# Attention's probabilities times values in plain float32, two key blocks in the two column halves of the array

## The chip, the core and the metric

One core of a Trainium2 chip runs the whole layer as one program. The metric is the device time of one execution in microseconds. The kernel before took 1462.4 us in the median of three runs (1460.74 to 1462.71). Engines are named as in the profile: PE is TensorE (PEld its weight loads), DVE is VectorE, ACT is ScalarE, POOL is GpSimd, SP is SyncE, which issues most DMAs.

## The reference, cut to what matters

The layer normalises its input, projects it once, and feeds two groups of heads: a gated delta rule (8 heads, chunks of 64 tokens) and multi-head latent attention (8 heads). Their outputs go through one output projection; a squared-ReLU MLP, a gated per-layer embedding and a final norm follow. There are 1024 tokens and 1024 channels, all float32. The change lies in the attention group:

```python
def blocked_causal_attention(q, k, v):          # 8 heads, S = 1024, dq = 96, dv = 64
    ...
    def block(args):                            # one block of 128 queries
        q_blk, start = args
        s = jnp.einsum('bhqd,bhkd->bhqk', q_blk, k, preferred_element_type=jnp.float32) * scale
        q_idx = start + jnp.arange(Q_BLOCK)
        s = jnp.where(key_idx[None, :] <= q_idx[:, None], s, -jnp.inf)
        pr = jax.nn.softmax(s, axis=-1).astype(v.dtype)
        return jnp.einsum('bhqk,bhkd->bhqd', pr, v)
```

The values `v` are the last 64 of the 128 columns that each head gets from the normalised latent (128 wide) times `w_kv_b`.

## The kernel before, in words

**Precision.** Large products run in float32r, a rounded form that the array takes in one pass. An operand is held as two float32r tiles, its rounded part ("hi") and the remainder ("lo"): ACT casts to the hi part and DVE subtracts it from the source for the lo part (`evac_split`, L177 to L180). `three` (L212 to L215) adds hi x hi, hi x lo and lo x hi. Small products (the delta rule's 64 x 64 ones, L610 and L838, and the decay matrix, L482) are plain float32, which the profile shows as two records a product.

**Order.** The program up to the MLP is written as named steps; the string `STEPS` (L65 to L92) lists them in the order in which they are traced, each step asserts that the steps it needs are done (L1460 to L1465), and the framework then plans the order on each engine from that priority with a timeline of its own, and places the waits. Buffers in SBUF are slots of 128 x 1024 float32 in five groups (`SLOTS`, L33; `HOMES`), so a step may also wait for a slot. PSUM is cut into four groups of banks (`BANKS`, L34): `a` has four, `p` two, `c` one, `o` one; `TAGS` says which tile takes which.

**Values.** `value_block(v, b)` (L989, steps `vb*` for heads 0 to 3 and `vc*` for heads 4 to 7) makes the values of four heads for 128 keys, 128 x 256 in PSUM. Even and odd heads are evacuated apart: per block two casts on ACT (L999) and two subtractions on DVE (L1000) fill a 128 x 512 tile, in which each head has 128 columns: hi beside lo, in an order that alternates from head to head. There are eight such buffers of 1024 columns.

**Scores.** A unit `u` is a head and a half of the queries (`hh = u // 2`, `g = u % 2`). `scores_block(u, i)` (L1079, steps `s{u}_{i}`) computes one block of 128 queries against all keys up to it: three matmuls a chunk into a `ps_s` bank (L1093 to L1095), the causal mask as a fourth (L1097), the row maximum on DVE (L1098), and exp on ACT with the row sum (L1105). The probabilities, not yet divided by the sum, lie as rows in `pn`.

**Probabilities times values.** `values_part(u, kb)` (L1110, steps `v{u}_{kb}`) takes one block of 128 keys: up to four transposes on PE put the block's probabilities, 128 keys x 512 queries, in a `pt_p` bank (L1119; tag `p`, two banks); blocks on the diagonal have 384, 256 or 128 queries. `evac_split` makes the hi and the lo part (L179, L180, into a `phl` slot), and two float32r matmuls add them into `po_a` (L1124, L1125; tag `o`, one bank). The 128 weight columns are hi and lo of the values, so one half of `po_a`'s partitions collects the products with hi and the other half those with lo. Half 0 of the queries has 4 key blocks, half 1 has 8: 96 steps in all. `values_end(u)` (L1127, steps `ve{u}`) adds the two halves: ACT copies one into `oT` (L1134) and DVE adds the other (L1135).

**Around it.** The steps of attention alternate in `STEPS` with the delta rule's outputs (`oa*`, `ob*`), the per-layer embedding (`ei*`, `eo*`), the head weights and rotary parts (`wn*`, `qn*`, `kn*`, `ro*`, `kp*`), loads, and at the end the first half of the output projection (`pa*`). The MLP and the gate follow, from 650 us on mostly matmuls.

Of the kernel before, what the change touches and what calls it, by code (L numbers as in the profile page):

```python
# [64 lines left out]
STEPS = """  # L65
ldx0 ldm0 start ldx2 ldx1 ldx7 ldx3 ldm1 mixcol ldm2 nx0 nx1 ldm3 ldx5 tx0_3 nx2 nx3 tx0_7 ldx4 tx0_0 tx0_1 tx1_6
tx0_5 tx0_4 columns tx1_7 tx1_1 spm0 spm2 nx5 tx0_2 masks spm3 tx1_0 spm1 tx0_6 tx1_4 nx7 ldx6 tx1_3 tx1_2 tx1_5
misc2 nx4 nx6 tx2_5 misc0 misc1 tx2_0 la00 tx2_2 tx2_1 wl7 tx2_3 misc3 tx2_7 tx2_4 tx2_6 misc6 wl4 misc5 misc4 misc7
gates ip4 cv4 wl5 ssk0_0 ssk0_1 ip5 dec0 dec1 cv5 wl0 ssk1_1 wl6 ip7 ssk1_0 wl1 ip6 cv7 dec3 wl2 ssk3_0 dec2 cv6
ssk2_1 wl10 ssk2_0 gk1 ssk3_1 cvals ip1 rotary cv1 cunit ip0 gk0 cv0 ssq0_0 ssq0_1 uu1 ip2 gk2 uu2 gk3 uu0 uu3 wl3  # L70
sub sub0 ssq1_1 sub1 la11 sub2 sub3 sub4 sub5 sub6 sub7 sub8 sub9 xout ssq1_0 cv2 ssq2_1 wl8 wl9 ssq2_0 ip3 cv3 wl13
qout0 ip8 la10 cv8 rv0_0 rv0_1 kbd1_0 ga3 ga2 ssq3_0 qout1 wl11 ip9 cv9 kbd3_0 kbd2_0 tl0 kbd0_1 ga1 ga0 tm0 ip11
tn0 ip10 wl12 kbd1_1 rv1_0 tl1 tm1 kbd0_0 mw0 cv10 tl2 tl3 ip12 cv12 tn1 mw1 kbd3_1 kbd2_1 ssq3_1 rv2_0 rv1_1 tm2
tn2 cv11 ip13 cv13 rv3_1 tm3 tn3 mw2 mw3 rv3_0 mu0 sc0 rv2_1 mu3 mu1 wl15 mu2 sc1 sc2 sc3 wl14 ip15 qout2 ip14 cv14
la01 lt0_2 sc4 lt1_1 lt0_0 sc5 cv15 lt0_1 sc6 lt1_0 sc7 sc8 sc9 sc10 wv0 vb1 wpe qp0 vb0 qp1 sc11 vb3 rq8 vb2 lt1_2
rkey sc12 sc13 sc14 qout3 ol6 qp7 qr00 qp2 vb6 wn0 kn0_1 vb5 ol0 vb4 kn0_0 sc15 ol2 ol3 qn0_0 qp4 vb7 ol1 kp3 oa0
qp5 oa1 kp0 ob0 qp6 qp3 qn0_1 qr01 qr11 oa2 ro0_0 s0_1 qr10 s0_2 s0_3 ro0_1 s0_0 v0_0 v0_1 v0_2 s1_2 s1_0 s1_1 v0_3
ve0 s1_3 v1_0 v1_1 v1_2 v1_3 v1_4 kp1 s2_0 v1_5 kp2 v1_6 v1_7 ve1 ob1 ob2 s2_2 oa3 s2_1 ol4 oa4 ob3 s2_3 ob4 s3_1
ol5 s3_0 oa6 v2_0 s3_3 v2_1 v2_2 oa5 ob6 s3_2 v2_3 wn1 qn1_0 ro1_0 qn1_1 kn1_1 ve2 v3_0 v3_1 kn1_0 ro1_1 v3_2 v3_3
v3_4 s4_2 s4_1 fa0 ol7 s4_0 oa7 s5_2 s4_3 v3_5 v3_6 v3_7 ve3 v4_0 v4_1 v4_2 s5_1 fb0 s5_0 s6_2 s5_3 v4_3 ob5 s6_1  # L80
ve4 v5_0 kp5 s7_1 v5_1 v5_2 v5_3 v5_4 v5_5 v5_6 wv1 vc1 s6_3 ob7 ro2_0 s7_2 v5_7 s7_0 vc0 plew ei0 ei1 eo1 eo0 s6_0
h2 ve5 v6_0 v6_1 v6_2 wn2 kn2_0 v6_3 vc4 vc5 vc3 s7_3 vc7 ve6 v7_0 v7_1 v7_2 v7_3 qn2_0 vc6 vc2 v7_4 fa1 ei2 v7_5
qn2_1 kp4 s8_3 kn2_1 s8_1 eo2 ro2_1 v7_6 s8_2 s8_0 kp7 s9_3 s10_3 s9_1 s9_0 v7_7 ve7 v8_0 fb1 v8_1 v8_2 v8_3 s9_2
ve8 v9_0 v9_1 v9_2 v9_3 v9_4 ei3 s10_0 eo3 s10_2 s10_1 s11_1 s11_0 ei4 v9_5 v9_6 v9_7 ro3_0 ve9 s11_2 eo4 v10_0
v10_1 v10_2 v10_3 ve10 s11_3 ei5 ro3_1 eo5 wn3 qn3_0 kn3_0 v11_0 kn3_1 kp6 v11_1 v11_2 v11_3 v11_4 fa2 s12_2 qn3_1
ei6 s12_1 s12_0 v11_5 v11_6 v11_7 ei7 y0 ve11 s12_3 v12_0 v12_1 v12_2 v12_3 s13_3 eo6 ve12 s13_2 s13_1 eo7 fb2 s13_0
v13_0 v13_1 v13_2 s14_1 v13_3 v13_4 y2 v13_5 s14_3 v13_6 v13_7 ve13 s14_2 s14_0 v14_0 v14_1 y1 v14_2 v14_3 ve14 wo0
s15_0 s15_1 h6 s15_3 s15_2 v15_0 wo1 wo2 v15_1 wo3 y4 y5 y3 fa3 v15_2 v15_3 v15_4 v15_5 v15_6 h3 h4 pa4 y6 v15_7
ve15 fb3 wo4 h7 pa3 rsy h0 wo5 h5 wo6 pa0 y7 pa5 pa7 pa6 wo7 h1 wu0 pb3 pa2 pb2 nh2 nh3 pb0 nh0 pb7 pa1 uo0 pb1 nh1 th0_1
pb4 nh7 wu1 pb6 nh6 th0_0 th0_2 nh4 pb5 nh5 th0_3   th1_1 th1_0  th1_2  th1_3    # L90
 
"""  # L92
# [23 lines left out]
def hybrid_block(ctx: ExitStack, tc: tile.TileContext, x, p, positions, mix_norm_w, w_in, conv_w,  # L116
# [872 lines left out]
    def value_block(v, b):  # L989

        pv = pp_("pv", b)[:, :256]
        three(pv, *at_block(cT, 2, b), *wt_["v", v][0], True, True)
        vt = tile_(f"V{v}{b // 2}", "V", F32R)[:, (b % 2) * 512:(b % 2 + 1) * 512]
        pvv = pv.rearrange("q (r e d) -> q r e d", e=2, d=C)
        vv = vt.rearrange("q (r c) -> q r c", c=256)
        for e in range(2):
# [2 lines left out]
            nc.scalar.copy(out=vh, in_=pvv[:, :, e])  # L999
            nc.vector.tensor_tensor(out=vl, in0=pvv[:, :, e], in1=f(vh), op=ALU.subtract)  # L1000
# [107 lines left out]
    po_ = {}  # L1108

    def values_part(u, kb):  # L1110
        hh, g = u // 2, u % 2
# [4 lines left out]
        i0 = max(0, kb - 4 * g)
        pt = pp_("pt_p")
        for i in range(i0, 4):
            nc.tensor.transpose(pt[:, i * P:(i + 1) * P], pn_view(u, i)[:, kb * P:(kb + 1) * P], ident)  # L1119
# [4 lines left out]
        nc.tensor.matmul(po[:, cs], vt, ph[:, cs], start=(kb == 0), stop=False)  # L1124
        nc.tensor.matmul(po[:, cs], vt, pl[:, cs], start=False, stop=(kb == nkb - 1))  # L1125

    def values_end(u):  # L1127

        hh, g, po = u // 2, u % 2, po_[u]
# [4 lines left out]
        nc.scalar.copy(out=ov, in_=po[oth])  # L1134
        nc.vector.tensor_tensor(out=ov, in0=po[rows], in1=ov, op=ALU.add)  # L1135
# [487 lines left out]
```

## Time and profile before

| what | value |
|---|---|
| median of three runs | 1462.4 us |
| the profiled execution's own time | 1459.25 us |
| its span, first to last instruction | 1457.5 us |
| mean granted TensorE clock | 0.972 |
| PE busy | 1380.4 us, 95% of the span |
| DVE busy | 1007.5 us, 69% |
| ACT busy | 662.8 us, 45% |
| POOL busy | 307.4 us, 21% |
| first and last matmul of `po_a` | 416.6 and 645.5 us |

A row of a group reads: line, engine, operation, output<-input, shape, count, then busy us and mean ns of one, then the engine's idle time just before these instructions and what ended it. A row of the timeline or of the chain of waits begins with start and length in us. Matmul records are pipelined and their ends are modelled, so two records may overlap; the distance between two starts is what a matmul costs the array. PE is a matmul, PEld its weight load.

### The profile page before, as it was taken

The numbers are of one execution on the slowest core, as the hardware profiler recorded it, in microseconds if no ns is written. First come the engines' busy times: TensorE is split into PE (matmuls) and PEld (weight loads), VectorE is DVE, ScalarE is ACT, GpSimd is POOL, SyncE is SP. The second block draws the span as 40 slices with busy tenths as digits, with TensorE's granted clock in tenths as the row PEclk, the third lists the DMA queues.
The fourth block names the chain that finished last, engine by engine and source line by source line (L and its number), as shares of the span: only waits on it lengthen the run. The fifth ranks groups of instructions, "written<-read, shape, count | busy, mean of one in ns | idle before, by whom it ended". The sixth has DMA issues, their size and how long they took to land.

```text
span 1457.5 us, 22314 instructions
## 1 busy us (share of the span) xinstructions
PE 1380.4 (95%) x8575; PEld 1130.7 (78%) x8575; DVE 1007.5 (69%) x1617; ACT 662.8 (45%) x1169; POOL 307.4 (21%) x417
## 2 busy tenths in 40 slices
PE   5999968999899999999989999999999999999897
PEld 4877847887677777888767888878887888888786
DVE  5567499545679687764697877778758775765464
ACT  6444210322357788842554544445534333333442
POOL 5412196321243511231510000000000000001410
PEclk9999988997889999999989999999999999999999
DMA  6112514423222423453224444443686423534411
GB/s 214 49 54 59 131 58 130 85 81 86 59 66 65 140 82 106 152 196 130 88 66 151 159 159 159 159 137 125 214 333 230 159 96 126 183 116 134 170 44 58
DMA packets 133590, 182.54 MB, mean 125 GB/s; under 512 B 38896, under 2 KB 88188, under 8 KB 133484
## 3 DMA queue, kind: packets, MB, share of 16 engines
q1 hardware_dynamic: 131900, 176.72, 37.3%
q0 software_dynamic: 1424, 4.14, 1.0%
q8 instruction: 67, 1.10, 0.3%
q14 instruction: 39, 0.32, 0.1%
q10 hardware_dynamic: 160, 0.27, 0.0%
HBM read 122.99 MB, written 58.10 MB: 124 GB/s over the span
## 4 chain that ended last, share of the span: by engine, by line
PE 47%; DVE 11%; DMA 8%; ACT 6%; issue 3%; POOL 1%; SPq 1%; DVEq 0%; POOLq 0%; ACTq 0%
DMA i_d<-D 4%; PE dmo L214 3%; PE dme L214 3%; PE dmo L215 3%; PE dme L215 3%; PE dme L213 3%; PE dmo L213 3%; DMA dar<-i_d 2%; PE pgt L215 2%; PE pgt L213 2%; PE pgt L214 2%; PE um L215 2%; PE um L214 2%; PE um L213 2%; PE pt_p L1119 1%
## 5 line engine op out<-in xcount | busy, mean ns | idle before, releaser
L1495 DVE TENSOR_TENSOR dal<-dar,dah 128x1024 fp32r<-128x1024 f32 x56 | 68.5, 1224 | 74.4 <-issue 32.1
L1544 POOL DMA_DIRECT2D rowg<-in_ple_gate_norm_w x1 | 0.6, 644 | 505.4 <-DVE dbs L1499 505.4
L214 PE MATMUL dme<-dbl,dah 128*128 128x512 f32 x256 | 99.7, 390 | 0.0
L215 PE MATMUL dme<-dbh,dal 128*128 128x512 f32 x256 | 99.4, 390 | 0.0
L213 PE MATMUL dme<-dbh,dah 128*128 128x512 f32 x256 | 99.2, 390 | 0.0
L1494 ACT CAST dah<-dar 128x1024 fp32r<-128x1024 f32 x56 | 58.8, 1050 | 62.0 <-DMA dar<-i_d 59.5
L1501 ACT CAST dbh<-dbs 128x1024 fp32r<-128x1024 f32 x40 | 42.1, 1053 | 90.1 <-DVE dbs L1499 45.6
L214 PE MATMUL dmo<-dbl,dah 128*128 128x512 f32 x192 | 74.4, 390 | 1.8 <-DVE dbl L1502 1.8
L215 PE MATMUL dmo<-dbh,dal 128*128 128x512 f32 x192 | 74.3, 390 | 0.0
L213 PE MATMUL dmo<-dbh,dah 128*128 128x512 f32 x192 | 72.8, 390 | 0.0
L180 DVE TENSOR_TENSOR phl<-pt_p,phl 128x512 fp32r<-128x512 f32 (+1 forms) x96 | 51.8, 550 | 17.8 <-ACT phl L179 16.8
L1098 DVE TENSOR_REDUCE stat<-ps_s 128x1 f32<-128x384 f32 (+5 forms) x96 | 51.5, 551 | 16.4 <-PE ps_s L1097 9.7
L213 PEld LDWEIGHTS dme<-dbh,dah 128*128 128x128 f32 x256 | 48.1, 188 | 10.0
L214 PEld LDWEIGHTS dme<-dbl,dah 128*128 128x128 f32 x256 | 48.1, 188 | 9.9
L215 PEld LDWEIGHTS dme<-dbh,dal 128*128 128x128 f32 x256 | 48.1, 188 | 9.9
L213 PE MATMUL um<-uc,t52h 128*128 128x512 f32 x128 | 51.4, 402 | 3.5 <-DVE Cb L1420 2.7
L179 ACT CAST phl<-pt_p 128x512 fp32r<-128x512 f32 (+1 forms) x96 | 44.5, 480 | 21.9 <-PE pt_p L1119 19.5
L1502 DVE TENSOR_TENSOR dbl<-dbs,dbh 128x1024 fp32r<-128x1024 f32 x40 | 48.9, 1222 | 6.7 <-ACT dbh L1501 6.4
L214 PE MATMUL um<-uc,t52h 128*128 128x512 f32 x128 | 50.8, 397 | 2.6 <-DVE uc L1282 2.6
L214 PE MATMUL um<-uc,t34h 128*128 128x512 f32 x128 | 50.7, 396 | 0.7 <-DVE uc L1282 0.7
L213 PE MATMUL um<-uc,t34h 128*128 128x512 f32 x128 | 50.9, 398 | 0.0
L215 PE MATMUL um<-uc,t34l 128*128 128x512 f32 x128 | 50.4, 393 | 0.0
(789 smaller groups left out, 4258.0 us busy)
## 6 DMA issues: line engine op xcount, KB each, us to landing
dar<-i_d SPq DMA_DIRECT2D x56, 512.0 KB, 3.8
i_d<-D SPq DMA_DIRECT2D x80, 256.0 KB, 3.9
wu<-in_w_up SPq DMA_DIRECT2D x32, 512.0 KB, 4.7
x<-in_x SPq DMA_DIRECT2D x8, 512.0 KB, 9.8
h<-in_x SPq DMA_DIRECT2D x8, 512.0 KB, 4.5
ep_d<-et SPq DMA_DIRECT2D x8, 512.0 KB, 2.8
yr<-y_d SPq DMA_DIRECT2D x8, 512.0 KB, 5.8
h_d<-h SPq DMA_DIRECT2D x8, 512.0 KB, 2.6
```

The lines of the kernel that those rows point to most:

```text
L179: nc.scalar.copy(out=hi, in_=src)
L180: nc.vector.tensor_tensor(out=lo, in0=src, in1=f(hi), op=ALU.subtract)
L213: nc.tensor.matmul(outp, ah, bh, start=first, stop=False)
L214: nc.tensor.matmul(outp, ah, bl, start=False, stop=False)
L215: nc.tensor.matmul(outp, al, bh, start=False, stop=last)
L1098: nc.vector.tensor_reduce(out=st[:, c:c + 1], in_=ps[c], axis=AX.X, op=ALU.max, negate=True)
L1119: nc.tensor.transpose(pt[:, i * P:(i + 1) * P], pn_view(u, i)[:, kb * P:(kb + 1) * P], ident)
L1494: nc.scalar.copy(out=ah, in_=raw)
L1495: nc.vector.tensor_tensor(out=al, in0=raw, in1=f(ah), op=ALU.subtract)
L1501: nc.scalar.copy(out=bh, in_=s_)
L1502: nc.vector.tensor_tensor(out=bl, in0=s_, in1=f(bh), op=ALU.subtract)
L1544: nc.gpsimd.dma_start(out=rowg, in_=ple_gate_norm_w[0].partition_broadcast(P))
```

## The change

The values are kept once, as plain float32: `value_block` copies 256 columns from PSUM with one ACT instruction into a tile that holds all eight heads of two key blocks (four buffers of 1024 columns instead of eight). `values_part` takes two key blocks at a time. It transposes both, each into its own `pt_p` bank; ACT copies the first and DVE the second to SBUF as they are, without split; then one plain float32 matmul per block with 64 weight columns follows. The first block's product goes to one half of `po_a`'s partitions, the second's to the other half, by the start partition of the output, so each occupies one half of the array's columns. The transposes and the number of columns that move through the array per block are as before. `values_end` is as before, but for the first half of the queries its add leaves out the first 128 columns, to which the second block of a pair has nothing to give. Of the steps `v{u}_{kb}` those with even `kb` remain, 48 instead of 96; in `STEPS` each stands where the odd one of its pair stood. The rest of the list keeps its order.

```diff
@@ value_block
-        vt = tile_(f"V{v}{b // 2}", "V", F32R)[:, (b % 2) * 512:(b % 2 + 1) * 512]
-        pvv = pv.rearrange("q (r e d) -> q r e d", e=2, d=C)
-        vv = vt.rearrange("q (r c) -> q r c", c=256)
-        for e in range(2):
-            vh = vv[:, :, e * 192:e * 192 + C]
-            vl = vv[:, :, 64 + e * 64:64 + e * 64 + C]
-            nc.scalar.copy(out=vh, in_=pvv[:, :, e])
-            nc.vector.tensor_tensor(out=vl, in0=pvv[:, :, e], in1=f(vh), op=ALU.subtract)
-        V[v, b] = vt
+        o_ = b % 2 * 512 + v * 256
+        nc.scalar.copy(out=tile_(f"V{b // 2}", "V")[:, o_:o_ + 256], in_=pv)
+
+    def value_of(hh, kb):
+        o_ = kb % 2 * 512 + hh * C
+        return tl[f"V{kb // 2}"][:, o_:o_ + C]
@@ values_part
-        i0 = max(0, kb - 4 * g)
-        pt = pp_("pt_p")
-        for i in range(i0, 4):
-            nc.tensor.transpose(pt[:, i * P:(i + 1) * P], pn_view(u, i)[:, kb * P:(kb + 1) * P], ident)
-        cs = slice(i0 * P, 512)
-        ph, pl = hl(slot("phl", "phl", F32R))
-        evac_split(pt[:, cs], ph[:, cs], pl[:, cs])
-        vt = V[hh // 4, kb][:, hh % 4 * P:(hh % 4 + 1) * P]
-        nc.tensor.matmul(po[:, cs], vt, ph[:, cs], start=(kb == 0), stop=False)
-        nc.tensor.matmul(po[:, cs], vt, pl[:, cs], start=False, stop=(kb == nkb - 1))
+        pT = slot("phl", "phl")
+        parts = []
+        for j in range(2):
+            i0 = max(0, kb + j - 4 * g)
+            pt = pp_("pt_p")
+            for i in range(i0, 4):
+                nc.tensor.transpose(pt[:, i * P:(i + 1) * P], pn_view(u, i)[:, (kb + j) * P:(kb + j + 1) * P], ident)
+            cs = slice(i0 * P, 512)
+            ph = pT[:, j * 512 + i0 * P:(j + 1) * 512]
+            if j:
+                nc.vector.tensor_copy(out=ph, in_=pt[:, cs])
+            else:
+                nc.scalar.copy(out=ph, in_=pt[:, cs])
+            parts.append((cs, ph))
+        for j, (cs, ph) in enumerate(parts):
+
+            half = (hh + 1 + j) % 2
+            nc.tensor.matmul(po[half * C:(half + 1) * C, cs], value_of(hh, kb + j), ph, start=(kb == 0),
+                             stop=(kb == nkb - 2))
@@ values_end
         nc.scalar.copy(out=ov, in_=po[oth])
-        nc.vector.tensor_tensor(out=ov, in0=po[rows], in1=ov, op=ALU.add)
+
+        c0 = 0 if g else P
+        nc.vector.tensor_tensor(out=ov[:, c0:], in0=po[rows, c0:], in1=ov[:, c0:], op=ALU.add)
@@ steps
-        for kb in range(4 * g + 4):
-            step(f"v{u}_{kb}", *(f"s{u}_{i}" for i in range(4)), f"v{'bc'[hh // 4]}{kb}", *([f"v{u}_{kb - 1}"] if kb else []),
+        for kb in range(0, 4 * g + 4, 2):
+            step(f"v{u}_{kb}", *(f"s{u}_{i}" for i in range(4)), *(f"v{'bc'[hh // 4]}{kb + j}" for j in range(2)),
+                 *([f"v{u}_{kb - 2}"] if kb else []),
                  *([f"ve{u - 1}"] if u and not kb else []))(lambda u=u, kb=kb: values_part(u, kb))
-        step(f"ve{u}", f"v{u}_{4 * g + 3}")(lambda u=u: values_end(u))
+        step(f"ve{u}", f"v{u}_{4 * g + 2}")(lambda u=u: values_end(u))
```

More of the change, by code (lines that the diff above doesn't have):

```diff
@@ L65 @@
 STEPS = """
[L66 to L90, printed above, removed]
+ldx0 ldm0 start ldx2 ldx1 ldx7 ldx3 ldm1 mixcol ldm2 nx0 nx1 ldm3 ldx5 tx0_3 nx2
@@ new lines @@
+nx3 tx0_7 ldx4 tx0_0 tx0_1 tx1_6 tx0_5 tx0_4 columns tx1_7 tx1_1 spm0 spm2 nx5 tx0_2 masks
+spm3 tx1_0 spm1 tx0_6 tx1_4 nx7 ldx6 tx1_3 tx1_2 tx1_5 misc2 nx4 nx6 tx2_5 misc0 misc1
+tx2_0 la00 tx2_2 tx2_1 wl7 tx2_3 misc3 tx2_7 tx2_4 tx2_6 misc6 wl4 misc5 misc4 misc7 gates
+ip4 cv4 wl5 ssk0_0 ssk0_1 ip5 dec0 dec1 cv5 wl0 ssk1_1 wl6 ip7 ssk1_0 wl1 ip6
+cv7 dec3 wl2 ssk3_0 dec2 cv6 ssk2_1 wl10 ssk2_0 gk1 ssk3_1 cvals ip1 rotary cv1 cunit
+ip0 gk0 cv0 ssq0_0 ssq0_1 uu1 ip2 gk2 uu2 gk3 uu0 uu3 wl3 sub sub0 ssq1_1
@@ new lines @@
+sub1 la11 sub2 sub3 sub4 sub5 sub6 sub7 sub8 sub9 xout ssq1_0 cv2 ssq2_1 wl8 wl9
+ssq2_0 ip3 cv3 wl13 qout0 ip8 la10 cv8 rv0_0 rv0_1 kbd1_0 ga3 ga2 ssq3_0 qout1 wl11
+ip9 cv9 kbd3_0 kbd2_0 tl0 kbd0_1 ga1 ga0 tm0 ip11 tn0 ip10 wl12 kbd1_1 rv1_0 tl1
+tm1 kbd0_0 mw0 cv10 tl2 tl3 ip12 cv12 tn1 mw1 kbd3_1 kbd2_1 ssq3_1 rv2_0 rv1_1 tm2
+tn2 cv11 ip13 cv13 rv3_1 tm3 tn3 mw2 mw3 rv3_0 mu0 sc0 rv2_1 mu3 mu1 wl15
+mu2 sc1 sc2 sc3 wl14 ip15 qout2 ip14 cv14 la01 lt0_2 sc4 lt1_1 lt0_0 sc5 cv15
+lt0_1 sc6 lt1_0 sc7 sc8 sc9 sc10 wv0 vb1 wpe qp0 vb0 qp1 sc11 vb3 rq8
@@ new lines @@
+vb2 lt1_2 rkey sc12 sc13 sc14 qout3 ol6 qp7 qr00 qp2 vb6 wn0 kn0_1 vb5 ol0
+vb4 kn0_0 sc15 ol2 ol3 qn0_0 qp4 vb7 ol1 kp3 oa0 qp5 oa1 kp0 ob0 qp6
+qp3 qn0_1 qr01 qr11 oa2 ro0_0 s0_1 qr10 s0_2 s0_3 ro0_1 s0_0 v0_0 s1_2 s1_0 s1_1
+v0_2 ve0 s1_3 v1_0 v1_2 kp1 s2_0 v1_4 kp2 v1_6 ve1 ob1 ob2 s2_2 oa3 s2_1
+ol4 oa4 ob3 s2_3 ob4 s3_1 ol5 s3_0 oa6 s3_3 v2_0 oa5 ob6 s3_2 v2_2 wn1
+qn1_0 ro1_0 qn1_1 kn1_1 ve2 v3_0 kn1_0 ro1_1 v3_2 s4_2 s4_1 fa0 ol7 s4_0 oa7 s5_2
+s4_3 v3_4 v3_6 ve3 v4_0 s5_1 fb0 s5_0 s6_2 s5_3 v4_2 ob5 s6_1 ve4 kp5 s7_1
@@ new lines @@
+v5_0 v5_2 v5_4 wv1 vc1 s6_3 ob7 ro2_0 s7_2 v5_6 s7_0 vc0 plew ei0 ei1 eo1
+eo0 s6_0 h2 ve5 v6_0 wn2 kn2_0 v6_2 vc4 vc5 vc3 s7_3 vc7 ve6 v7_0 v7_2
+qn2_0 vc6 vc2 fa1 ei2 v7_4 qn2_1 kp4 s8_3 kn2_1 s8_1 eo2 ro2_1 s8_2 s8_0 kp7
+s9_3 s10_3 s9_1 s9_0 v7_6 ve7 fb1 v8_0 v8_2 s9_2 ve8 v9_0 v9_2 ei3 s10_0 eo3
+s10_2 s10_1 s11_1 s11_0 ei4 v9_4 v9_6 ro3_0 ve9 s11_2 eo4 v10_0 v10_2 ve10 s11_3 ei5
+ro3_1 eo5 wn3 qn3_0 kn3_0 kn3_1 kp6 v11_0 v11_2 fa2 s12_2 qn3_1 ei6 s12_1 s12_0 v11_4
+v11_6 ei7 y0 ve11 s12_3 v12_0 v12_2 s13_3 eo6 ve12 s13_2 s13_1 eo7 fb2 s13_0 v13_0
@@ L92 @@
+s14_1 v13_2 y2 v13_4 s14_3 v13_6 ve13 s14_2 s14_0 v14_0 y1 v14_2 ve14 wo0 s15_0 s15_1
+h6 s15_3 s15_2 wo1 wo2 v15_0 wo3 y4 y5 y3 fa3 v15_2 v15_4 h3 h4 pa4
+y6 v15_6 ve15 fb3 wo4 h7 pa3 rsy h0 wo5 h5 wo6 pa0 y7 pa5 pa7
+pa6 wo7 h1 wu0 pb3 pa2 pb2 nh2 nh3 pb0 nh0 pb7 pa1 uo0 pb1 nh1
+th0_1 pb4 nh7 wu1 pb6 nh6 th0_0 th0_2 nh4 pb5 nh5 th0_3 th1_1 th1_0 th1_2 th1_3
 """
```

## The prediction, made before the changed kernel ran

> **What bounds the kernel now.** I read the page's engine shares and slices first, then the busy time of each engine by stretch, then the groups and single starts on the array.
>
> ```profile
> span 1457.5 us, 22314 instructions
> PE 1380.4 (95%) x8575; PEld 1130.7 (78%) x8575; DVE 1007.5 (69%) x1617; ACT 662.8 (45%) x1169; POOL 307.4 (21%) x417
> ...
> PE   5999968999899999999989999999999999999897
> ```
>
> PE's row stands at 9 nearly throughout (a slice is 36.4 us), so by the page TensorE bounds the kernel. The attention steps s*, v*, ve* lie between 405 and 646 us, slices 12 to 18. In the columns below (stretch, its length, busy time and count of PE, PEld, DVE, ACT, POOL; clock, DMA) that stage stands first, then two of its stretches, then one behind it.
>
> ```profile
> 405.00:646.00 241.00, 230.21 (x1610) 186.73 (x1609) 190.54 (x369) 181.47 (x467) 72.52 (x107) 0.97 0.37 120
> ```
> ```profile
> 450.00:480.00 30.00, 28.58 (x282) 22.75 (x280) 27.64 (x54) 22.81 (x61) 13.53 (x24) 1.00 0.19 54
> 510.00:540.00 30.00, 27.68 (x166) 22.60 (x165) 27.42 (x60) 23.98 (x68) 4.08 (x6) 1.00 0.24 73
> ...
> 650.00:690.00 40.00, 40.00 (x186) 33.38 (x186) 14.94 (x22) 6.90 (x11) 8.74 (x10) 1.00 0.36 131
> ```
>
> From 650 us on PE is busy without a gap and DVE and ACT have little to do: whatever the attention stage gains or loses arrives undiminished at the end. Inside the stage PE looks 96% busy, but DVE is at 92% and 91% in two stretches, and PE's figure flatters it:
>
> ```profile
> 96.26 0.40 PE L234 MATMUL acc_p<-uT,w7h 128*128 128x512 f32 x1
> 96.49 0.40 PE L236 MATMUL acc_p<-uT,w7l 128*128 128x512 f32 x1
> ...
> 557.39 0.39 PE L1124 MATMUL po_a<-phl,V 128*128 128x256 f32 x1
> 557.85 0.39 PE L1125 MATMUL po_a<-phl,V 128*128 128x256 f32 x1
> ...
> 574.30 0.88 PE pt_p L1119 x8
> ```
>
> These are rows of the timeline (start, length), the last one of the chain of waits. Two float32r matmuls of 512 columns start 0.23 us apart, though each record is 0.40 long; eight transposes take 0.88, 0.11 each. So the pair at 557.39, with 256 columns worth 0.115, lost 0.34 us that PE's row counts as busy (L1125 needs DVE's low part). By these spacings the stage's matmuls (scores 8 heads x 4608 columns x 3, 49.7 us; 288 transposes, 31.7; po_a, 33.1 below; the fill-in steps oa, ob, ei, eo, qn, kn, vc, pa and the sums, some 85) stream for about 200 us: an estimate, leaving some 40 of 241 in which the array stands. The page shows only 10.8 of these (241 less 230.2); where, these groups say:
>
> ```profile
> L1093 PE MATMUL ps_s<-kh,qh 96*128 96x512 f32 (+5 forms) x95 | 39.0, 411 | 2.6 <-ACT pn L1105 1.3 <-ACT pn8a L1105 0.6 <-DVE ql L1039 0.3
> L1124 PE MATMUL po_a<-phl,V 128*128 128x512 f32 (+1 forms) x96 | 36.1, 378 | 2.5 <-ACT phl L179 2.2 <-ACT pe L1215 0.2
> L1125 PE MATMUL po_a<-phl,V 128*128 128x512 f32 (+1 forms) x96 | 36.0, 380 | 1.0 <-DVE phl L180 0.9
> ...
> L1119 PE MATMUL pt_p<-ident,pn 128*128 128x128 f32 x208 | 33.8, 276 | 1.5 <-DVE ql L1039 0.9 <-ACT pn L1105 0.5
> ```
>
> po_a 3.5, ps_s 2.6, pt_p 1.5. Scaled by 40/10.8 that is about 13, 10 and 5.5 us of standing array.
>
> **The change part by part.** *The products.* Removed: 192 float32r matmuls, per half (hi, lo):
>
> ```profile
> L1124 PE MATMUL po_a<-phl,V x96: 221/390/506, 416.6 to 645.5; 128*128 128x512 f32 x48, 128*128 128x384 f32 x16, 128*128 128x256 f32 x16, 128*128 128x128 f32 x16
> ```
>
> At 0.23 per 512 columns: 2 x (48 x 0.23 + 16 x 0.1725 + 16 x 0.115 + 16 x 0.0575) = 33.1 us. Added: 96 plain float32 matmuls with 64 weight columns, in 48 pairs (16 of widths 512 and 512, 16 of 512 and 384, 16 of 256 and 128). The plain float32 product of this kernel is L482, and L610 and L838 write column halves by turns:
>
> ```profile
> L482 PE MATMUL pe<-R,striL 128*128 128x512 f32 x16 | 7.7, 592 | 0.0
> ...
> 94.71 1.02 PE L482 MATMUL pe<-R,striL 128*128 128x512 f32 x2
> 95.66 0.27 PE L610 MATMUL pk<-kT 64*64 64x64 f32 x2
> ...
> 95.77 0.22 PE L610 MATMUL pk<-kT 64*64 64x64 f32 x2
> 95.92 0.50 PE L233 MATMUL acc_p<-uT,w7h 128*128 128x512 f32 x1
> ...
> 341.41 0.45 PE L838 MATMUL pds<-Uv,kd 64*64 64x64 f32 x8
> ```
>
> L482 runs 8 products as 16 records, so one product is two passes; two records take 1.02 together, one by itself 0.59, so a pass of 512 columns costs 0.43. Of L610 both halves' first passes lie within 0.27 us from 95.66, both second ones within 0.22 from 95.77: the halves run together. L838 agrees: eight passes in 0.45, against 0.65 if each 64-column pass (0.43 x 64/512 = 0.054) waited for the one before (7 x 0.054 + the last one's 0.27). So a pair costs two passes of its wider member: 16 x 0.86 + 16 x 0.86 + 16 x 0.43 = 34.4. Bounds: one half after the other gives 61.9.
>
> *Changing the array's shape.* L482's second record starts at 95.14, L610 at 95.66: 0.52 where a pass is 0.43. Back: 95.77 to 95.92 is 0.15 where a pass is 0.054. About 0.09 us each way. Each pair stands between full-width transposes and scores, so 48 x 0.18 = 8.6 us. Bounds: 0, since no row has 128 rows with column halves, and 0.2 per pair. With it the products cost 43.0, that is +9.9; bounds +1.3 and +38.
>
> [...]
>
> *The evacuations.* Removed: 96 casts on ACT, 96 subtractions on DVE. Added: 48 copies on each, ACT of the first block, DVE of the second.
>
> ```profile
> L180 DVE TENSOR_TENSOR phl<-pt_p,phl 128x512 fp32r<-128x512 f32 x48 | 32.6, 682 | 5.5 <-ACT phl L179 4.9
> L180 DVE TENSOR_TENSOR phl<-pt_p,phl 128x384 fp32r<-128x384 f32 x16 | 8.8, 550 | 2.3 <-ACT phl L179 2.2
> L180 DVE TENSOR_TENSOR phl<-pt_p,phl 128x128 fp32r<-128x128 f32 x16 | 4.6, 286 | 2.0 <-ACT phl L179 1.7
> L842 DVE COPY S<-pds 128x128 f32<-128x128 f32 x2 | 0.5, 292 | 4.0 <-PE pds L838 4.0
> L1000 DVE TENSOR_TENSOR V<-pv,V 128x128 fp32r<-128x128 f32 x32 | 8.4, 280 | 1.2 <-ACT V L999 0.9
> ```
> ```profile
> L179 ACT CAST phl<-pt_p 128x512 fp32r<-128x512 f32 x48 | 27.4, 586 | 9.9 <-PE pt_p L1119 9.4
> L179 ACT CAST phl<-pt_p 128x256 fp32r<-128x256 f32 x16 | 6.0, 372 | 9.2 <-PE pt_p L1119 7.4 <-PE po_a L1125 1.6
> L999 ACT CAST V<-pv 128x128 fp32r<-128x128 f32 x32 | 7.7, 266 | 20.7 <-PE pv L215 17.8 <-DVE V L1000 2.8
> L1009 ACT COPY qpe<-pv_q 128x256 f32<-128x256 f32 x8 | 3.0, 372 | 10.3 <-PE pv_q L215 10.1
> ```
> ```profile
> L179 ACT CAST phl<-pt_p 128x512 fp32r<-128x512 f32 (+1 forms) x96 | 44.5, 480 | 21.9 <-PE pt_p L1119 19.5
> L180 DVE TENSOR_TENSOR phl<-pt_p,phl 128x512 fp32r<-128x512 f32 (+1 forms) x96 | 51.8, 550 | 17.8 <-ACT phl L179 16.8
> L1098 DVE TENSOR_REDUCE stat<-ps_s 128x1 f32<-128x384 f32 (+5 forms) x96 | 51.5, 551 | 16.4 <-PE ps_s L1097 9.7 <-PE ps_s L1095 5.9
> L1135 DVE TENSOR_TENSOR oT<-po_a,oT 64x512 f32<-64x512 f32 x15 | 10.3, 686 | 1.4 <-ACT oT L1134 1.2
> ...
> L1102 DVE TENSOR_TENSOR stat<-stat 128x1 f32<-128x1 f32 x32 | 9.9, 309 | 0.3
> ```
>
> A DVE copy of 128 columns (0.292) costs what the subtraction does (0.286), so I take the subtraction's rows: 16 x 0.682 + 16 x 0.550 + 16 x 0.286 = 24.3 instead of 51.8, -27.5; lower bound, ACT's speed, some 3 us less. ACT: 32 x 0.586 + 16 x 0.372 = 24.7 instead of 44.5, -20. The values' own split goes: 32 subtractions (-9.0 on DVE), and 16 copies of 256 columns for 32 casts (-2.5 on ACT), half of each before 405 us. The second add of values_end loses 128 columns in eight cases: -1. Also the wait ACT before DVE inside each block (16.8 us of DVE's idle time) disappears.
>
> ```profile
> 390.00:405.00 15.00, 10.96 (x144) 9.04 (x143) 13.27 (x32) 7.47 (x19) 6.94 (x11) 0.85 0.02 6
> ```
>
> The earlier half of V's split meets a DVE that is 88% busy just ahead of the stage.
>
> *What waits where.* A pair holds both pt_p banks; its first product waits for ACT's copy, its second for DVE's, and behind them on PE queue the next transposes and scores, for which exp and the maxima wait. An odd step moves to its pair's place; no DMA moves, no queue is passed. V takes four buffers instead of eight.
>
> *What that is worth.* None of it is on PE, so only the standing 40 us can shrink. At po_a there are half as many waits and no subtraction behind the cast: I take half of 13, -6.5. ps_s and pt_p (15.5 together) wait on DVE and ACT queues that lose 17% (27.5 + 4.5 + 1 of 190) and 12% (20 + 1.3 of 181): I take a quarter, -4. Where the pair has to wait anyway, its entry into the halves costs nothing; I assume 4 cases in 10, 0.4 x 48 x 0.09 = -1.7, and if they never coincide this is lost. V's split before 405 us: a third of its 5.8, -1.9. Sum: 9.9 - 6.5 - 4 - 1.7 - 1.9 = **-4.2 us**. Bounds of the relief: 0, and 22.
>
> The profiled execution took 1459.25 (span 1457.5 and 1.75 around it), 3.15 under the median of 1462.4. 1459.25 - 4.2 = 1455.05; with 3.15, **1458.2**.
>
> **The rivals.**
>
> *A, the array sets the stage's pace.* At each of the 48 pairs it pays for passes of 0.43 and two changes of shape, and the time that DVE and ACT are given stays unused, since the array stands for reasons of order and latency and not of load. Then only +9.9 counts: 1459.25 + 9.9 + 3.15 = **1472**. For it: the array's work is the largest of the three already, and behind 650 us nothing is given back. It decides once the standing time shrinks by less than 9.9 of 40. Against it: DVE at 92% and 91%.
>
> *B, DVE and ACT set the pace.* DVE's attention work by the rows above is 51.8 + 51.5 + 9.9 + 10.3 = 123.5 us, PE's 49.7 + 31.7 + 33.1 = 114.5; after it 95 against 124. If the array then stands 20 us instead of 40: 9.9 - 20 - 1.9 = -12, **1450**. Against it: the fill-in steps are PE's for the most part, and with them PE leads.
>
> *C, the halves don't overlap at 128 rows.* 61.9 + 8.6 - 33.1 = +37.4, less the same relief of 14.1: **1486**. For it nothing in the trace but that all halves seen are 64 rows high. [...] L838, whose halves share their rows, disagrees.
>
> *D, the change of order eats the difference.* The order on each engine is planned anew: **1462**, within a microsecond or two.
>
> **How the numbers follow.** Forecast (own range 1454 to 1462) 0.38; A 0.26; B 0.18; C 0.07; D 0.11. Three runs lie within 2 us, so 0.2% (2.9 us) is what a measurement tells from no change. Faster: B 0.17 and 0.28 of the forecast, 0.45. Same: 0.10 of the forecast, D's 0.11, 0.02 of A and B, 0.23. Slower: A 0.25, C 0.07: 0.32. Range: from B with 2 us more to A: 1448 to 1473; C and the far ends of the bounds (-20 and beyond +10 with no relief) are left out.
>
> **What would show it.** Right: in the pair, the second half's first pass starts some 0.01 us behind the first half's, passes are 0.43 apart, 0.09 more on either side; phl on DVE and ACT falls to some 24 us each; fewer idle us before po_a. Wrong: passes of the two halves in single file (C); the array standing as long as before (A) or less than 20 us (B); differences outside 340 to 650 us.

## The result, and the profile after

The changed kernel takes 1488.0 us in the median of four runs (1486.2 to 1489.7); the kernel before, beside it, 1462.6 (1460.7 to 1466.5). The ratio is 1.0170, 95% interval 1.0146 to 1.0195: 25 us slower, where 4 us faster were forecast. ScalarE and VectorE were relieved, and the kernel became slower all the same. Header and slices of the changed kernel's page:

```profile
span 1488.0 us, 22099 instructions
...
PE 1406.7 (95%) x8575; PEld 1117.0 (75%) x8575; DVE 978.2 (66%) x1537; ACT 644.8 (43%) x1105; POOL 307.0 (21%) x417
...
PEclk9999978998899899999999999999999999999999
```

DVE is busy 29 us less than before and ACT 18 less, PE 26 more. The groups of the two copies and of the products:

```profile
L1133 ACT COPY phl<-pt_p 128x512 f32<-128x512 f32 (+1 forms) x48 | 24.8, 516 | 28.2 <-PE pt_p L1127 19.1 <-issue 8.2 <-PE po_a L1138 0.5
L1131 DVE COPY phl<-pt_p 128x384 f32<-128x384 f32 (+2 forms) x48 | 24.4, 509 | 37.2 <-PE pt_p L1127 37.0
L1138 PE MATMUL po_a<-phl,V 128*64 128x512 f32 (+2 forms) x192 | 61.7, 521 | 1.2 <-ACT pe L1232 1.2
```

The copies cost 24.8 and 24.4 us, as forecast (24.7 and 24.3), and ahead of them the two engines now stand idle for 28 and 37 us, ACT's for the larger part and DVE's nearly all until PE's transposes. The array hardly waits for them: 1.2 us ahead of `po_a`. And yet the attention stage is longer: `po_a` runs from 418.4 to 668.3 us (416.6 to 645.5 before), and the MLP's first matmul starts 27 us later (743.7 for 716.5). Where that time goes shows in PE's timeline of the changed kernel (start, length, and at the end of the line the number of records). Records of `po_a` with no other matmul between them are called a stretch here:

```profile
418.39 1.07 PE L1138 MATMUL po_a<-phl,V 128*64 128x512 f32 x4
419.39 0.33 PE L1127 MATMUL pt_p<-ident,pn0a 128*128 128x128 f32 x1
...
428.59 1.07 PE L1138 MATMUL po_a<-phl,V 128*64 128x512 f32 x2
429.59 0.66 PE L1127 MATMUL pt_p<-ident,pn 128*128 128x128 f32 x4
430.18 1.07 PE L1138 MATMUL po_a<-phl,V 128*64 128x512 f32 x2
431.18 0.66 PE L1127 MATMUL pt_p<-ident,pn 128*128 128x128 f32 x4
...
599.95 1.94 PE L1138 MATMUL po_a<-phl,V 128*64 128x512 f32 x8
601.82 0.38 PE L1097 MATMUL ps_s<-kh,qh 96*128 96x256 f32 x1
```

At 418.39 a whole pair, four records, takes 1.00 us up to the next matmul. At 428.59 one product alone, two records, takes 1.00 us as well, because its partner comes only at 430.18: between them the planned order has the first transposes of the next pair. At 599.95 two pairs side by side take 1.87. So the halves do run together here (the pair's 1.00 us are those of one product), but only where they stand next to each other in PE's order. Counted over the trace, the 192 records form 59 stretches, and 42 of them hold a single product. From its first start to the next other matmul, the 59 stretches take 58.0 us; with 0.09 each for the entry into the halves, 63.3, where the forecast had 43.0 for 48 whole pairs. In the kernel before, whose products take the whole width (128*128) like the transposes beside them, so that no entry is added, the stretches take 45.6 us by the same measure, for 33.1 by the spacings.

### The profile page after: what moved, and what is told of

Its sections match the earlier page's. It is cut to its first block, busy times and chain, and to the rows that moved or that the text cites. A ratio compares the mean times of both kernels' runs of the same rounds, so it can differ in the third digit from the quotient of the medians.

```text
span 1488.0 us, 22099 instructions
## 1 busy us (share of the span) xinstructions
PE 1406.7 (95%) x8575; PEld 1117.0 (75%) x8575; DVE 978.2 (66%) x1537; ACT 644.8 (43%) x1105; POOL 307.0 (21%) x417
## 4 chain that ended last, share of the span: by engine, by line
PE 51%; DVE 10%; DMA 7%; ACT 4%; issue 3%; POOL 1%; SPq 0%; DVEq 0%; POOLq 0%; ACTq 0%
DMA i_d<-D 4%; PE po_a L1138 3%; PE dme L221 3%; PE dme L222 3%; PE dme L220 3%; PE dmo L221 3%; PE dmo L222 3%; PE dmo L220 3%; PE pt_p L1127 2%; PE pgt L220 2%; PE pgt L222 2%; PE pgt L221 2%; PE um L222 2%; PE um L220 2%; PE um L221 2%
## 5 line engine op out<-in xcount | busy, mean ns | idle before, releaser
L1138 PE MATMUL po_a<-phl,V 128*64 128x512 f32 (+2 forms) x192 | 61.7, 521 | 1.2 <-ACT pe L1232 1.2
L220 PE MATMUL um<-uc,t67h 128*128 128x512 f32 x128 | 50.3, 393 | 0.0
L222 PE MATMUL um<-uc,t52l 128*128 128x512 f32 x128 | 49.7, 399 | 0.3 <-DVE t52l L1385 0.3
```

The lines of the kernel that those rows point to most:

```text
L220: nc.tensor.matmul(outp, ah, bh, start=first, stop=False)
L222: nc.tensor.matmul(outp, al, bh, start=False, stop=last)
L1138: nc.tensor.matmul(po[half * C:(half + 1) * C, cs], value_of(hh, kb + j), ph, start=(kb == 0), stop=(kb == nkb - 2))
```

## The experiments

The theory taken from this ("order"): the separated pairs lose some 20 us, and what stays is rival A, the array's pace. The rival ("the halves themselves"): plain float32 and the changes of shape are dearer than their spacings show, and the order is not to blame. Every ratio below is to the kernel before on the same chip.

### Pairs tied together

```diff
-        for j, (cs, ph) in enumerate(parts):
-            half = (hh + 1 + j) % 2
-            nc.tensor.matmul(po[half * C:(half + 1) * C, cs], value_of(hh, kb + j), ph, start=(kb == 0),
-                             stop=(kb == nkb - 2))
+        with tc.high_priority():
+            for j, (cs, ph) in enumerate(parts):
+                half = (hh + 1 + j) % 2
+                m_ = nc.tensor.matmul(po[half * C:(half + 1) * C, cs], value_of(hh, kb + j), ph, start=(kb == 0),
+                                      stop=(kb == nkb - 2))
+                if j == 0:
+                    tc.add_manual_dep(m_.ins, second.ins.name,
+                                      mybir.DependencyInfo(mybir.DependencyClass.Sync, mybir.DependencyReason.DATA),
+                                      reason="both halves together")
```

> The changed kernel, with the two products of a pair kept side by side: the first waits for VectorE's copy as well as for ScalarE's, so that all 48 pairs follow each other directly on TensorE's queue (in the changed kernel 42 of the 59 stretches of po_a work hold one product alone). Theory 'order': a lone product of 512 columns costs about 1.0 us plus 0.09 us of entry where a pair of them costs about 1.05 plus 0.09, so some 20 us of the changed kernel's time are lost to separated pairs; expected 1466 to 1473 us if the freed time of VectorE and ScalarE is worth little (rival A's 1472), 1455 to 1462 if it is worth what the forecast took. The new wait of the first product may cost up to 0.3 us a pair, 14 us at worst, and would show as waits at po_a. Theory 'the halves themselves' (the shape changes or plain float32 cost it, not the order): no gain, 1485 to 1491 us.

`second` is VectorE's copy. Measured: 1475.8 us, ratio 1.0114 (1.0086 to 1.0142). All pairs are adjacent; their stretches take 41.6 us and 40 entries of 0.09, 45.2 together instead of 63.3. The time falls by 8 us, less than half of that, and is 3 us above the range that the order theory gave. The rival's 1485 and more is out. The new wait is small: the array waits 1.0 us in all at `po_a` for VectorE's copy.

### Products one pair later

```diff
+        if kb:
+            products(u, kb - 2, t_.ins)
+        late[u, kb] = parts
...
+    def products(u, kb, after=None):
...
+        with tc.issue_after(after) if after is not None else nullcontext(), tc.high_priority():
+            for j, (cs, ph) in enumerate(parts):
...
```

> As the kernel with tied pairs, but the products of a pair are issued one pair later, behind the transposes of the next pair, so that the copies of VectorE and ScalarE run while TensorE transposes the next pair. Theory 'order', with the wait at po_a worth something: 3 to 10 us faster than the tied kernel, 1455 to 1468 us, with the idle time before po_a below 5 us. Theory 'order', but the array never lacks work (rival A): within 3 us of the tied kernel. Theory 'the halves themselves': 1485 us or more, like the changed kernel.

`t_` is the last transpose of the pair at hand; the body of the loop is that of the tied pairs, and a unit's last pair comes ahead of its closing add. Measured: 1469.3 us, ratio 1.0071 (1.0044 to 1.0098). Its rows in the timeline, and the group of its products:

```profile
475.25 0.79 PE L892 MATMUL pav<-Uv,A 64*64 64x64 f32 x18
475.97 1.07 PE L1151 MATMUL po_a<-phl,V 128*64 128x512 f32 x4
476.97 0.68 PE L892 MATMUL pav<-Uv,A 64*64 64x64 f32 x14
```
```profile
L1151 PE MATMUL po_a<-phl,V 128*64 128x512 f32 (+2 forms) x192 | 43.0, 507 | 1.2 <-ACT pe L1250 1.2
```

The pair takes 1.00 again, now with both products in it, and the group is busy 43.0 us instead of 61.7. The products cost the array 40.7 + 40 x 0.09 = 44.3 by the spacings, 19.0 less than in the changed kernel; the time falls by 0.0099 of 1459, 14.4 us. The intervals of the two ratios (up to 1.0098, from 1.0146) are apart. Against the tied kernel 6.5 us are gained, in the 3 to 10 that were expected if the wait is worth something, but the time is 1 us above the 1468 of that expectation, and these two intervals overlap.

Of the 25 us, tying brings back 8 and deferring 14; in both kernels the order is also planned anew. The traces, one of each kernel, show it in the stage itself: from the first matmul of the scores to the MLP's first there are 312.4 us before, 340.4 in the changed kernel, 323.1 in the tied and 319.5 in the deferred one, which wins back 21 of 28. So the separated pairs are the larger part of the loss; its exact size is not settled, since the times and the traces differ.

### Full width, no halves

```diff
-        o_ = kb % 2 * 512 + hh * C
-        return tl[f"V{kb // 2}"][:, o_:o_ + C]
+        o_ = kb % 2 * 512 + hh // 2 * P
+        return tl[f"V{kb // 2}"][:, o_:o_ + P]
...
-            nc.tensor.matmul(po[half * C:(half + 1) * C, cs], value_of(hh, kb + j), ph, start=(kb == 0),
-                             stop=(kb == nkb - 2))
+            nc.tensor.matmul(po[:, cs], value_of(hh, kb + j), ph, start=(kb + j == 0), stop=(kb + j == nkb - 1))
```

> The changed kernel with the products over the full width of the array: the weights are the values of two heads (128 columns), each product writes all 128 rows of po_a and only the half that belongs to the head is used. No column halves, no change of shape, the copies as in the changed kernel (the closing step takes a maximum of a half with itself where the changed kernel adds two halves, the same number of instructions). 96 products of two passes each, none shared: 61.9 us by the pass of 0.43 us. Theory 'order': the changed kernel spends 58.0 us in its po_a stretches and 5.3 us in entries, so this one lands within 5 us of it, 1482 to 1491 us. Theory 'the halves themselves' (changes of shape dearer than 0.09 us each way, or waits that they bring): clearly faster than the changed kernel, 1465 to 1478 us.

Measured: 1486.9 us, ratio 1.0196 (1.0162 to 1.0230), against the changed kernel's 1.0170: no difference that these intervals tell, as the order theory had it. Its stretches take 62.4 us for the changed kernel's 63.3. With most pairs apart, the halves win back about what their changes of shape cost. In this kernel a pass of 512 columns takes 0.43 us to the next one or to a transpose; in the kernel with deferred pairs the last pass of a pair takes 0.523 to the next full-width matmul, and a pair starts 0.202 after the last transpose, where full-width plain float32 starts after 0.109. Both ways that is 0.093, the forecast's 0.09. A third piece stands in no term of the forecast: in halves the second pass of a stretch, at 512 columns, starts 0.48 after the first, 0.05 more than 0.43; later passes keep 0.43.

### VectorE's relief by itself

```diff
-        evac_split(pt[:, cs], ph[:, cs], pl[:, cs])
+        nc.scalar.copy(out=ph[:, cs], in_=pt[:, cs])
...
-        nc.tensor.matmul(po[:, cs], vt, pl[:, cs], start=False, stop=(kb == nkb - 1))
+        nc.tensor.matmul(po[:, cs], vt, ph[:, cs], start=False, stop=(kb == nkb - 1))
```

> The kernel before, without VectorE's 96 subtractions that make the low part of the probabilities; the second product of each block reads the high part again, so TensorE's work is unchanged and the low part is left out of the result. It prices the relief of VectorE alone: 51.8 us of its work go. The forecast's way of costing the relief (a smaller wait at po_a, a quarter of the waits at ps_s and pt_p) gives 8 to 12 us faster than before, 1450 to 1455 us. Rival B: 15 us or more faster. Rival A (the time given to VectorE stays unused): within 3 us of before, 1460 to 1466 us.

Measured: 1466.1 us, ratio 1.0048 (1.0027 to 1.0069): slower, not faster, though 52 us of DVE's work are gone and the array's is the same. At `po_a` the relief does show: its stretches take 38.8 us in this trace for 45.6 before, with the same passes. Two kernels ask why it doesn't reach the end.

```diff
+        c1 = slice(i0 * P, i0 * P + 16)
+        low = nc.vector.tensor_tensor(out=pl[:, c1], in0=pt[:, c1], in1=f(ph[:, c1]), op=ALU.subtract)
...
+        m_ = nc.tensor.matmul(po[:, cs], vt, ph[:, cs], start=False, stop=(kb == nkb - 1))
+        tc.add_manual_dep(m_.ins, low.ins.name,
+                          mybir.DependencyInfo(mybir.DependencyClass.Sync, mybir.DependencyReason.DATA),
+                          reason="as before")
```

> The kernel before with the subtraction cut to its first 16 columns; the second product reads the high part again but still waits for that subtraction, so every wait of the kernel before is kept and only VectorE's time shrinks (96 instructions, by some 40 us; the low part is left out of the result). It asks whether the 7 us that the kernel without subtraction lost against before come from the missing wait (another order on TensorE) or from the relief. Forecast's way of costing the relief: 6 to 10 us faster than before. Rival A (relief unused): within 3 us of before. If an idle VectorE itself does harm: 4 to 8 us slower, as without the subtraction.

Measured: 1474.3 us, ratio 1.0091 (1.0058 to 1.0124), with every wait kept: slower by more than any of the theories allowed, though its interval overlaps that of the kernel without the wait. What this kernel does not keep is the order. Both kernels are planned anew, and in their traces PE's order leaves that of before as soon as `po_a` starts (before has three matmuls of the scores between the first two products; in the other two these follow each other). So neither parts the relief from a new plan. The third kernel prices a new plan by itself.

```diff
-s0_0 v0_0 v0_1 v0_2 s1_2 s1_0 s1_1 v0_3 ve0 s1_3
+s0_0 v0_0 v0_1 s1_2 s1_0 s1_1 v0_2 v0_3 ve0 s1_3
```

This is the first unit; the others are treated in the same way.

> The kernel before with nothing changed but the list of steps: each even step of the values stands directly ahead of its odd one, at the place where the changed kernel has the pair. The same instructions, planned anew. Rival D (the change of order does it): 5 us or more away from before. The forecast, A, B: within 3 us of before. What this one moves is also a measure of how much a new plan alone moves the time.

Measured: 1466.1 us, ratio 1.0056 (1.0032 to 1.0081). With no work changed at all, this new order costs 8 us. Rival D is real, and its price is not the nothing that the forecast gave it. It also means that the 7 us of the kernel without the subtraction may be the price of its plan: these runs show that the relief brought no gain, not that it is worth nothing by itself.

### The high part alone

```diff
-        evac_split(pt[:, cs], ph[:, cs], pl[:, cs])
+        nc.scalar.copy(out=ph[:, cs], in_=pt[:, cs])
...
-        nc.tensor.matmul(po[:, cs], vt, ph[:, cs], start=(kb == 0), stop=False)
-        nc.tensor.matmul(po[:, cs], vt, pl[:, cs], start=False, stop=(kb == nkb - 1))
+        nc.tensor.matmul(po[:, cs], vt, ph[:, cs], start=(kb == 0), stop=(kb == nkb - 1))
```

> The kernel before without the low part of the probabilities: no subtraction on VectorE and no second product, so one float32r product a block (the low part is left out of the result). TensorE loses half of the 33.1 us of its products, 16.6, VectorE loses 51.8. Rival A (TensorE sets the pace of the stage, one us of it is one us of time): 12 to 18 us faster than before, and 16 to 20 us faster than the kernel that leaves out the subtraction alone. Rival B (VectorE and ScalarE set the pace): that kernel would have shown it already, and taking the products away as well gives little more: within 5 us of it.

Measured: 1458.0 us, ratio 0.9995 (0.9973 to 1.0018). Against the kernel without the subtraction that is 0.0053 lower, 7.7 us for 16.6 us of the array's work; the intervals are apart. That lies between A's 16 to 20 and B's 5: array work counts in this stage, but here only by half. Two windows of the stage (404 to 480 and 480 to 510 us; columns as in the prediction) of before, then of the kernel without the subtraction, and the second window of this kernel tell where the rest goes:

```profile
404.00:480.00 76.00, 73.52 (x677) 58.57 (x673) 63.41 (x125) 53.74 (x142) 31.32 (x59) 0.93 0.25 70
480.00:510.00 30.00, 27.47 (x202) 22.07 (x201) 18.98 (x41) 22.60 (x59) 14.25 (x18) 1.00 0.50 150
```
```profile
404.00:480.00 76.00, 72.81 (x674) 58.93 (x671) 53.05 (x104) 56.78 (x151) 27.03 (x50) 0.99 0.23 66
480.00:510.00 30.00, 22.07 (x179) 18.44 (x179) 10.09 (x16) 13.86 (x36) 17.08 (x20) 0.68 0.50 139
```
```profile
480.00:510.00 30.00, 24.18 (x149) 19.31 (x150) 14.59 (x32) 17.68 (x41) 14.49 (x16) 0.72 0.43 129
```

Between 480 and 510 us the array of both kernels is short of work (22.1 and 24.2 us busy for 27.5) and its granted clock falls to 0.68 and 0.72, where before it has 1.00. To see who leads, each matmul outside `po_a` is weighed by the shortest spacing of its kind in before, and the time is taken at which before has done the same sum. By that estimate the kernel without the subtraction is some 5 us ahead of before at 480 us and 7 behind at 510 (the expectations below reckon 6 and 9); the one with the high part alone goes from 8 to 3 ahead, the one with the small subtraction from 0.5 ahead to 9.5 behind, the changed kernel from 6 to 13 behind. The kernel with only another order loses almost nothing there (3.4 behind, then 4.0). In these traces a lead is won first, and lost again in these 30 us.

### Two pairs in a row

```diff
-        if kb:
-            products(u, kb - 2, t_.ins)
+        if kb == 4:
+            products(u, 0, t_.ins)
```

> As the kernel with deferred pairs, but the products of two pairs in a row, behind the transposes of the second or third pair: 24 groups of four products in place of 48 of two, so 24 entries into the column halves and 24 exits fewer, the same passes. If each change of shape costs the array 0.09 us that nothing hides: 24 x 0.18 = 4.3 us faster than the deferred pairs, ratio to before about 1.004 (1465 where before is 1459). If the changes of shape are free or hidden: as the deferred pairs, ratio 1.007. If the four copies make the array wait: slower than that, with idle time before po_a above 3 us.

`products` now takes the pairs of four blocks; a unit's last two pairs come at its end. Measured: 1467.1 us, ratio 1.0045 (1.0023 to 1.0067), 0.0026 or 3.8 us below the deferred pairs, near the 4.3 expected; the two intervals overlap, so the time alone does not show it. The spacings do: 37.7 + 23 x 0.09 = 39.8 us for 44.3. The stretches fall from 40 to 23, by 17 and not by 24, since some of the deferred pairs already stood side by side.

### What makes the stretch from 480 to 510 us sparse

SP's queue in the kernel without the subtraction, then in before:

```profile
482.85 0.35 SPq L198 DMA_DIRECT2D wp0r<-in_w_ple_proj  x1
...
489.16 0.34 SPq L1147 DMA_DIRECT2D r_d<-rs__4963  x1
...
502.41 0.35 SPq L198 DMA_DIRECT2D wp1r<-in_w_ple_proj  x1
```
```profile
487.11 0.42 SPq L198 DMA_DIRECT2D wp0r<-in_w_ple_proj  x1
490.08 0.33 SPq L198 DMA_DIRECT2D wp1r<-in_w_ple_proj  x1
```

The first half of a weight leaves 4 us earlier than before, the second 12 us later, and the products `pe` that need both cannot fill the stretch. The first explanation: the transpose of the softmax sums (`pt_r`), which shares a bank with the delta rule, is late, and with it `r_d` and what follows.

```diff
-'pt_r': 'c'
+'pt_r': 'a'
```

> The kernel before with one small transpose (the reciprocal softmax sums of finish_a, four in all) written to a bank of group a instead of the single bank of group c, which the delta rule's outputs use too. In the kernel before that transpose ends in time (its transfer r_d leaves SP at 477 us, the weights wp0r and wp1r behind it at 487 and 490). Both theories: within 4 us of before. It is the control for the three kernels below.

> The kernel without the subtraction, with the same other bank for that transpose. By its trace TensorE is 6 us ahead of before at 480 us and 9 behind at 510: the transpose came behind the delayed delta rule on bank c, so r_d left at 489, wp1r at 502, TensorE lacked the work that needs them and its granted clock fell to 0.50 from 490 to 510 us. Theory 'the relief is won and lost again in this stretch': with the transpose freed the loss of 15 us between 480 and 510 shrinks to below 8, and the time falls by 5 to 10 us against the kernel without subtraction, to 3 to 6 us below before (ratio 0.996 to 0.998). Rival 'the stretch is only where it shows' (TensorE sets the pace, the lost time moves elsewhere): within 3 us of the kernel without subtraction, ratio 1.003 to 1.007.

> The kernel with two deferred pairs in a row, with the same other bank. By its trace it loses 7 us against before between 480 and 510 us, wp1r leaves at 508.6. Theory 'won and lost again': 3 to 7 us faster than without the other bank, ratio to before 1.000 to 1.002, which would be the best version of the change. Rival: ratio 1.003 to 1.006, as without it.

> The changed kernel, with the same other bank and nothing else. By its trace it loses 10 us against before between 480 and 510 us at granted clocks of 0.50 to 0.76; wp1r leaves at 516.7. Theory 'won and lost again': 4 to 9 us faster than the changed kernel, ratio to before 1.011 to 1.014; what is left is the lone products and the changes of shape. Rival: ratio 1.015 to 1.019, as the changed kernel.

Measured, as ratios in this order: 1.0047 (1.0026 to 1.0068), 1.0026 (1.0002 to 1.0051), 1.0063 (1.0039 to 1.0087) and 1.0170 (1.0145 to 1.0195). In the kernel without the subtraction `r_d` now leaves at 459.6 instead of 489.2 us, but `wp1r` still at 505.8, and the array's clock is at 0.50 from 500 to 515. No kernel gains what was expected, and the control loses 7 us, outside the 4 expected for it. Against this control, which shares its change of bank, the kernel without the subtraction is 3 us faster, with intervals that overlap. The explanation falls. The second: `wp1r` itself, whose slot waits for a transfer of the delta rule.

```diff
-'wp1r': 'r'
+'wp1r': 'g'
-'pt_r': 'c'
+'pt_r': 'a'
```

> The kernel without the subtraction, with the other bank for the transpose of the softmax sums and with wp1r in a slot of group g instead of r, so that its transfer does not wait for the delta rule's y_d. Theory 'late weights': wp1r leaves SP before 495 us (502.4 without), the pe products fill the stretch, the granted clock stays above 0.9 from 480 to 520 us, and the time falls to 1450 to 1455 us where before is 1459 (ratio 0.995 to 0.998). Rival 'only where it shows': ratio 1.002 to 1.006, and the array stands or slows elsewhere.

> The kernel with the high part alone (one product a block, no subtraction), with the same two changes of place. Without them it lost 10 us of its lead between 480 and 510 us and ended at a ratio of 0.9995. Theory 'late weights': 6 to 10 us faster than without, ratio 0.993 to 0.996. Rival: ratio 0.998 to 1.001.

> The changed kernel with the same two changes of place. Theory 'late weights': ratio to before 1.011 to 1.014 (1.017 without), no granted clock below 0.9 between 480 and 540 us; the lone products and the changes of shape stay. Rival: 1.015 to 1.019.

> The kernel with two deferred pairs in a row, with the same two changes of place. Theory 'late weights': 3 to 7 us faster than without them, ratio to before 1.000 to 1.002. Rival: 1.003 to 1.007.

Measured, in this order: 1.0034 (1.0014 to 1.0054), 1.0017 (0.9995 to 1.0039), 1.0167 (1.0136 to 1.0199) and 1.0061 (1.0038 to 1.0084). All four lie with the rival or above it. The kernel before with both moves was not run, so the price of the new plan in them is not known. The move itself worked; of the kernel without the subtraction:

```profile
490.79 0.85 SPq L198 DMA_DIRECT2D wp1r<-in_w_ple_proj  x1
```
```profile
480.00:510.00 30.00, 23.74 (x225) 19.97 (x225) 11.72 (x22) 18.03 (x45) 20.23 (x24) 0.79 0.36 116
```

`wp1r` leaves 12 us earlier, and the array is still only 23.7 us busy at a clock of 0.79. So the late weight was where the stretch shows, not its cause, or at most a small part of it. What makes the array run short there is open. Its longest single wait in this last kernel is 3.0 us for ScalarE's cast of `wv`, the weight of the values of heads 4 to 7; with the high part alone it is 4.2 us for the same cast, while before does not wait for it. The relieved array may simply arrive ahead of its next weights; no run tested that. No version that keeps the probabilities whole was faster than the kernel before.

## Why the prediction was wrong, point by point

**What bounds the kernel.** "Whatever the attention stage gains or loses arrives undiminished at the end" held: from the MLP's first matmul on, the two profiles differ by 3 us, and the loss lies in the stage. Of the 40 us of standing array, the 13 put down to `po_a` are borne out: its stretches take 45.6 us before for 33.1 by the spacings, 12.5 more. With deferred pairs they take 44.3 us, no more than before, although the passes and the changes of shape are dearer: the standing there is gone. What did not hold is that time won at one place shortens the stage. With deferred pairs it is still 7.1 us longer than before, so the array lost that time at other matmuls.

**The products.** This step failed: "a pair costs two passes of its wider member". It took the two products for neighbours in the array's queue. In the code they are; in the planned order 42 of 59 stretches hold one product alone, which pays its passes, its entry and its exit by itself. The term measured 63.3 us and not 43.0, 20.3 too little in the sum. With it the forecast's own sum gives 16 us slower; 25 were measured, so of the 14.1 us of relief about 5 are left, or a new plan took the rest. Where the pairs are kept together the forecast's term is right within 1.3 us: 44.3 measured for 43.0. That the halves overlap at 128 rows was right too: the first passes of a pair start at 418.390 and 418.397, its second passes at 418.770 (384 columns) and 418.871 (512), and the whole pair takes no longer than one product of 512 columns alone.

**Changing the array's shape.** Right in size for the way in and the way out: 0.093 each. The 0.05 between the first two passes was left out, though L610's rows in the prediction have it (95.66 to 95.77 is 0.11 for a pass of 0.054). The price was charged 48 times; with the pairs apart it falls due 59 times.

**The evacuations.** The copies are right to 0.1 us on both engines. VectorE's busy time as a whole fell by 29 us, where the forecast's terms add up to 37.5; that difference stays open.

**What waits where, and what that is worth.** The relief of 14.1 us (6.5 + 4 + 1.7 + 1.9) did not arrive as time, and this is the second step that failed. The 6.5 at `po_a` did come: 6.8 us in the kernel without the subtraction, 45.6 to 38.8. Yet that kernel, which takes away more of VectorE's work than the change does, is not faster than before. By its trace the array was some 5 us ahead by 480 us; from 480 to 510 it then ran short of work (busy 22.1 of 30 us, 27.5 before) at a granted clock of 0.68 (1.00 before). How much of this is the new plan, which alone costs 7 to 8 us in two other kernels, is not shown.

**The rivals.** A comes closest in time: with the pairs kept together, 1469.3 to 1475.8 us are its 1472. But the number is not proof of its sum, since a new order without any change of work costs 7 to 8 us (1.0047 and 1.0056), so the 10 us of the deferred pairs may be the 9.9 of the products with no relief, or a new order with some relief against the products. In the traces the stage, from the first matmul of the scores to the MLP's first, is 7.1 us longer with deferred pairs, and 2.4 and 3.4 longer with only a new plan: some of it is the plan, then, and the rest is less than A's 9.9. One trace of each does not part the two. B is out. C's time, 1486, is nearly the result, but by chance: the halves do overlap where they are neighbours (first passes 0.007 us apart), and its sum takes off 14 us of relief that there was not. D, set at "within a microsecond or two", is 7 to 8 us dearer than that.

**The signs to look for.** The second half's first pass 0.01 behind, 0.09 on either side, `phl` at 24 us each, fewer idle us before `po_a`: these came. Passes 0.43 apart came only from the second pass on. Not one of these signs could show the error, since they hold for a pair that is together and say nothing of one that is not. The sign that was missing from the list was the count of stretches.

## What to carry to other kernels

Two products in halves shared the array here only where they were neighbours in its planned order (1.00 us for an adjacent pair, 1.00 for one product alone), so a cost that rests on sharing is to be checked in that order, and the pair tied by a common wait (8 us here) or also issued behind the next block's transposes (14 us in all). Ahead of counting on relief, take the work away from the relieved engine alone and measure: in this stage, where the array is 96% busy, 52 us less of VectorE's time gave no faster kernel. And a kernel with a planned order needs a control that changes nothing but the plan, since its own price (7 to 8 us here) is as large as most effects looked for.
